# One ring of buffers for the high half, the low half and the raw form of a weight tile

## The chip, the cores and the metric

The kernel runs on 1 core of one Trainium2 chip. The metric is the device time of one execution in microseconds (us). Engines are named as the profile names them: PE is TensorE's matmul, PEld its weight load, DVE is VectorE, ACT ScalarE, POOL GpSimd, and SP is SyncE, which here only issues DMAs. A name with a q behind it (SPq, PEq) is the engine's sequencer, which waits for semaphores and issues DMAs.

## The reference

The kernel computes one layer of a streaming encoder trunk with D = 1024 for 2128 tokens (64 of a running stream, 16 meta tokens, 2048 of a prompt). Three branches (RWKV-7, S5, mLSTM) take their inputs from one combined projection:

```
P   = x @ w_in            columns shared out among the branches, their gates and the merge gates
y_b = branch_b(P columns) * silu(gate_b columns)              b in {rwkv7, s5, mlstm}
m   = sum_b sigmoid(P_merge_b + b_merge_b) * (y_b @ w_br_b)   w_br: 768, 512 and 768 rows of 1024
x   = LayerNorm(DN_ALPHA * x + m @ w_out)                     w_out: 1024 x 1024
```

Everything is float32. A product of two float32 matrices is made out of rounded parts: each operand is cut into a high part (the value rounded to the type fp32r) and a low part (the value less its high part), and three products are summed, high by high, high by low and low by high.

## The kernel before

**Weight tiles.** A weight tile is 128 columns of a weight matrix with all its rows, kept as 4, 6 or 8 k-tiles of 128 x 128 (kt below). `split_w` (line 393) makes its two parts. For each run of up to 4 k-tiles it takes three buffers: `raw`, into which SP loads the float32 columns (line 403), `hi`, which ACT writes by a rounding copy (line 404), and `lo`, which POOL writes by a subtraction (line 405). Each kind has its own ring, and the rings are counted in halves of a tile with 8 k-tiles: `WBUF` gives (3, 4) for the pool `wp` with the tag "w" (3 buffers for raw, 4 for hi, 4 for lo), and (2, 2) for the pool `gp` with the tag "g". A buffer holds 2 KB in each of 128 partitions, so the w rings take 22 KB of a partition and the g rings 12 KB.

**Token blocks.** The tokens go through five blocks: block 0 has 336 of them, the others 448 each. Each block runs 63 projections on the w rings (`proj`, which calls `load_w` at line 415 and `mm3` at 428) and 24 merge gates on the g rings (`gate_pass`, line 1499), each with kt = 8, that is 24 matmuls into one PSUM bank (tiles `d` for projections, `f` for gates). In block 0 (`first`) the tile comes from w_in by `split_w`, and hi and lo of each half are written to a DRAM buffer `wsp` (line 410, 256 KB each, so four writes for a tile). In blocks 1 to 4 `load_w` reads the four pieces back (line 424), into the hi and lo rings. `ml_gates` (line 840) builds a narrow tile on the w rings, with a raw buffer of its own, and the S5 branch loads four raw tiles of w_glu in each block into the w ring of raw buffers (line 1412).

**Merge.** `merge_pass` (line 1509) takes 768, 768 and 576 tokens. In each group it multiplies the branch outputs by w_br, 8 weight tiles each with kt = 6 (rw), 4 (s5) and 6 (ml), then by w_out, 8 tiles with kt = 8. Every one of these tiles is split afresh by `split_w`. In the last group w_out is gone through twice, for 320 and for 256 columns of tokens, so that 16 tiles are split there, with the layer norms beside them.

**What sets the order.** The branches of a block are Python generators, which `mix` steps with the weights of `MIXES` (line 1677); gate passes are given as work to fill in. From there a scheduler with a simulated timeline places the instructions of each engine, and pools hand out the buffers. All weight DMAs, raw, written and read back, are issued by SP in one queue, in order. A load into a ring waits until its buffer's last readers are done, and it keeps those behind it on SP waiting. DMAs on SP use eight semaphores in turn, so that a DMA can also wait for one eight places before it.

Of the kernel before, what the change touches and what calls it, by code (L numbers as in the profile page):

```python
# [9 lines left out]
F32 = mybir.dt.float32  # L10
F32R = mybir.dt.float32r
I32 = mybir.dt.int32
AF = mybir.ActivationFunctionType
ALU = mybir.AluOpType
# [5 lines left out]
KD = D // 128  # L20
# [63 lines left out]
def tile_trunk(ctx: ExitStack, tc: tile.TileContext, I, O, dbg=None, parts=("rw", "s5", "ml", "mg")):  # L84
    nc = tc.nc
    V, S, G, PE = nc.vector, nc.scalar, nc.gpsimd, nc.tensor
# [4 lines left out]
    dram = ctx.enter_context(tc.tile_pool(name="dram", bufs=1, space=DRAM))  # L91
    cst = ctx.enter_context(tc.tile_pool(name="cst", bufs=1))
    wp = ctx.enter_context(tc.tile_pool(name="wp", bufs=1))
# [13 lines left out]
    def pt(pool, shape, tag, dt=F32, bufs=None):  # L107
        uid[0] += 1
        kw = {} if bufs is None else {"bufs": bufs}
        return pool.tile(list(shape), dt, tag=tag, name=f"{tag}_{uid[0]}", **kw)  # L110
# [3 lines left out]
    def psum(shape, tag):  # L114
        return pt(ps, shape, tag, bufs=PSB[tag])
# [12 lines left out]
    def cut(t, off, shape):  # L128
        n = 1
        for x in shape[1:]:  # L130
            n *= x
        v = t[:shape[0], off:off + n]
        if len(shape) == 3:
            v = v.rearrange("p (a b) -> p a b", b=shape[2])
        elif len(shape) == 4:
            v = v.rearrange("p (a b c) -> p a b c", b=shape[2], c=shape[3])
        elif len(shape) == 5:
            v = v.rearrange("p (a b c d) -> p a b c d", b=shape[2], c=shape[3], d=shape[4])
        return v
# [240 lines left out]
    def load_x(b):  # L380
        for nm, j, e in (("xh", 0, nc.sync), ("xl", 1, nc.scalar)):
# [5 lines left out]

    w_in = I["w_in"][0].rearrange("(k p) c -> p k c", p=128)

    WBUF = {"w": (3, 4),  # L390
            "g": (2, 2)}

    def split_w(pool, src, kt, M, tag="w", keep=None):
        if keep is not None:
            wsp_d[keep] = pt(dram, (2, 2, 128, 4, 128), f"wsp{keep}")
        nr, nh = WBUF[tag]
        hi, lo = [], []
        for k in range(0, kt, 4):
            n = min(4, kt - k)
            h = pt(pool, (128, 4, 128), tag + "hi", F32R, bufs=nh)  # L400
            l = pt(pool, (128, 4, 128), tag + "lo", F32R, bufs=nh)
            raw = pt(pool, (128, 4, 128), tag + "raw", bufs=nr)
            nc.sync.dma_start(raw[:, :n, :M], src[:, k:k + n])
            S.copy(h[:, :n, :M], raw[:, :n, :M])  # L404
            G.tensor_tensor(l[:, :n, :M], raw[:, :n, :M], h.bitcast(F32)[:, :n, :M], ALU.subtract)  # L405
            hi += [h[:, m, :M] for m in range(n)]
            lo += [l[:, m, :M] for m in range(n)]
            if keep is not None:
                for j, t in enumerate((h, l)):
                    nc.sync.dma_start(wsp_d[keep][k // 4, j], t.bitcast(F32))  # L410
        return hi, lo

    wsp_d = {}

    def load_w(pool, off, first, tag="w"):
        nh = WBUF[tag][1]
        if first:
            wh, wl = split_w(pool, w_in[:, :, off:off + 128], KD, 128, tag, keep=off)
            return wh, wl
        hi, lo = [], []  # L420
        for k in range(0, KD, 4):
            for j, (nm, out) in enumerate((("hi", hi), ("lo", lo))):
                t = pt(pool, (128, 4, 128), tag + nm, F32R, bufs=nh)
                nc.sync.dma_start(t.bitcast(F32), wsp_d[off][k // 4, j])
                out += [t[:, m] for m in range(4)]
        return hi, lo

    def mm3(p, wh, wl, T):
# [7 lines left out]
    def proj(b, off):  # L436
        wh, wl = load_w(wp, off, b.first)
        p = psum((128, 512), "d")
        mm3(p[:, :b.T], wh, wl, b.T)
        return p  # L440
# [399 lines left out]
    def ml_gates(b):  # L840
        T = b.T
        nch = len(b.tiles)
        raw = pt(wp, (128, KD, 8), "wraw", bufs=WBUF["w"][0])
        nc.sync.dma_start(raw, w_in[:, :, O_MIF:O_MIF + 8])
        wh, wl = [], []
        for k in range(0, KD, 4):
            h = pt(wp, (128, 4, 128), "whi", F32R, bufs=WBUF["w"][1])
            l = pt(wp, (128, 4, 128), "wlo", F32R, bufs=WBUF["w"][1])
            for t in (h, l):
                G.memset(t.bitcast(F32)[:, :, 0:100], 0.0)  # L850
            for j in range(2):
                o = h[:, :, 32 * j:32 * j + 4]
                r = raw[:, k:k + 4, 4 * j:4 * j + 4]
                S.copy(o, r)
                S.copy(l[:, :, 32 * j:32 * j + 4], r)
                V.tensor_tensor(l[:, :, 64 + 32 * j:68 + 32 * j], r, o.bitcast(F32), ALU.subtract)
            wh += [h[:, m, 0:100] for m in range(4)]
            wl += [l[:, m, 0:100] for m in range(4)]
# [5 lines left out]
        li, lf, m, bb = (gr[k][:, :T] for k in ("li", "lf", "m", "b"))  # L864
# [451 lines left out]
    def s5_block(b, u_d, y_d):  # L1316
# [3 lines left out]
        for i in range(4):  # L1320
# [8 lines left out]
            for j in range(2):  # L1329
                w = cut(w5(), 0, (128, 2, 2, 128))  # L1330
# [38 lines left out]
            for q in range(4):  # L1369
                w = cut(w5(), 0, (128, 4, 128))  # L1370
                nc.sync.dma_start(w, s5wo_d[4 * i + q])
                m = []
# [3 lines left out]
                for ri in range(2):  # L1376
                    for a in range(2):
                        for g in range(2):
                            r = slice(64 * g, 64 * g + 64)
                            t = slice(64 * (a ^ g), 64 * (a ^ g) + 64)  # L1380
# [28 lines left out]
        wg = I["s5_w_glu"][0].rearrange("(k p) c -> p k c", p=128)  # L1409
        for i in range(4):  # L1410
            ch = slice(128 * i, 128 * i + 128)
            raw = pt(wp, (128, 4, 128), "wraw", bufs=WBUF["w"][0])
            nc.sync.dma_start(raw, wg[:, :, ch])
            p = psum((128, 512), "d")
            pv = p[:, :T].rearrange("p (s c) -> p s c", s=8)
            for k in range(4):
                PE.matmul(pv, raw[:, k], Gs[k], start=k == 0, stop=k == 3)  # L1417
            th = cut(sB(), 0, (128, 8, NC))
            S.activation(th, pv, AF.Tanh, scale=0.25, bias=hglu[:, i:i + 1])
            V.scalar_tensor_tensor(th, th, 1.0, Gs[i], ALU.add, ALU.mult)  # L1420
            sg = sB()
            nc.sync.dma_start(sg[:, :T], ys5_d[b.i][ch, :])
            s3 = sg[:, :T].rearrange("p (c s) -> p c s", s=8)
            V.scalar_tensor_tensor(s3, th.rearrange("p s c -> p c s"), 0.125, s3, ALU.mult, ALU.mult)
            nc.sync.dma_start(ys5_d[b.i][ch, :], sg[:, :T])
            yield
# [3 lines left out]
    def s5_stream(b):  # L1430
        for g in spend:
            yield from g
        d = yield from s5_proj(b)
        if b.first:
            yield from s5_setup()
            spend[:] = [s5_block(b, *d)]
        else:
            spend[:] = []
            yield from s5_block(b, *d)
# [69 lines left out]
    def merge_pass():  # L1509
# [58 lines left out]
        def branch_w(B, bi, d):  # L1568
            nm, yd, kt = BR[bi]
            th = pt(pool["th"], (128, TB), "th2", bufs=2)  # L1570
            for b, lo, o, m in seg[B]:
                nc.scalar.dma_start(th[:, o:o + m], g_d[b.i][D * bi + 128 * d:D * bi + 128 * d + 128, lo:lo + m])
            return split_w(wp, w_br[nm][:, :, 128 * d:128 * d + 128], kt, 128) + (th,)
# [178 lines left out]
```

## Time and profile before

| | us |
|---|---|
| median of 3 runs | 4247.48 |
| lowest, highest | 4238.52, 4260.57 |
| profiled execution | 4243.47 |
| its span in the trace | 4241.7 |

In the trace the stages are, by their windows: 0 to 100 us, start of block 0; 100 to 440 us, the larger part of block 0's weight tiles; 440 to 848 us, the end of block 0 and its change to block 1; 848 to 3600 us, blocks 1 to 4; 3600 us to the end, the merge. Busy times of PE are ends that are modelled, and matmuls follow each other closely, so the mean time of one matmul in a list is longer than its share of a row of matmuls; how long a weight tile takes PE is read from the chain of waits, which gives a time for a whole row of matmuls.

### The profile page before, as it was taken

How to read it: one execution, taken by the hardware profiler on the slowest of the kernel's cores; microseconds unless marked ns; L12 is line 12 of the kernel's file. 1: busy time of each engine (PE TensorE's matmuls, PEld its weight loads, DVE VectorE, ACT ScalarE, POOL GpSimd, SP SyncE). 2: the span in 40 equal slices, each digit the busy share in tenths (PEclk: the TensorE clock that was granted, in tenths of full speed). 3: DMA queues.
4: the chain of work that ended last, by engine and by line, in shares of the span. 5: the costliest groups of instructions: out<-in, count | busy, mean ns of one | idle time of the engine just before them, and what ended most of it. 6: DMA issues, size and time to landing. Idle time of an engine off the chain costs nothing.

```text
span 4241.7 us, 78557 instructions
## 1 busy us (share of the span) xinstructions
PE 3989.1 (94%) x27999; PEld 3427.6 (81%) x27999; DVE 2490.6 (59%) x8212; ACT 1208.0 (28%) x2655; POOL 662.9 (16%) x948
## 2 busy tenths in 40 slices
PE   6889789899999899999999999999999999999997
PEld 6778567688888778888888888878888787999997
DVE  6446886566456565556645645554665554457476
ACT  4434332232222222222322222222322222222222
POOL 5445321000000000001000000000000000233335
PEclk9999879899999899999999999999999999999999
DMA  8999647665665755656665656665566654666565
GB/s 257 332 271 320 197 136 224 175 181 187 194 211 183 226 161 175 197 181 209 196 223 165 193 173 203 178 205 189 171 202 192 168 170 132 202 194 197 156 181 165
DMA packets 803862, 834.91 MB, mean 197 GB/s; under 512 B 220246, under 2 KB 557374, under 8 KB 803470
## 3 DMA queue, kind: packets, MB, share of 16 engines
q1 hardware_dynamic: 725582, 756.61, 58.0%
q10 hardware_dynamic: 77888, 73.28, 5.8%
q8 instruction: 221, 3.62, 0.3%
q14 instruction: 171, 1.40, 0.1%
HBM read 633.92 MB, written 197.79 MB: 196 GB/s over the span
## 4 chain that ended last, share of the span: by engine, by line
PE 72%; DVE 11%; DMA 10%; SPq 2%; ACT 2%; issue 2%; POOL 1%; ACTq 0%; POOLq 0%; DVEq 0%
PE d L433 29%; PE f L433 10%; PE z L1562 7%; PE g L1562 3%; PE tr L591 2%; PE py L747 2%; PE py L744 1%; PE d L1417 1%; PE o L1011 1%; DMA ghi<-wsp 1%; DMA xT<-X 1%; DVE Ztmp L622 1%; PE tr L700 1%; PE py L734 1%; PE tr L708 1%
## 5 line engine op out<-in xcount | busy, mean ns | idle before, releaser
L433 PE MATMUL d<-xh,whi 128*128 128x448 f32 (+1 forms) x2520 | 945.9, 375 | 30.1 <-DVE zo L1092 7.7
L433 PE MATMUL d<-xh,wlo 128*128 128x448 f32 (+1 forms) x2520 | 932.4, 370 | 5.6 <-POOL wlo L405 5.1
L433 PE MATMUL d<-xl,whi 128*128 128x448 f32 (+1 forms) x2520 | 928.6, 369 | 0.0
L433 PEld LDWEIGHTS d<-xh,whi 128*128 128x128 f32 x2520 | 485.2, 193 | 86.3 <-issue 16.6
L433 PEld LDWEIGHTS d<-xh,wlo 128*128 128x128 f32 x2520 | 484.0, 192 | 55.3 <-POOL wlo L405 8.3
L433 PEld LDWEIGHTS d<-xl,whi 128*128 128x128 f32 x2520 | 485.0, 192 | 43.5 <-issue 9.1
L405 POOL TENSOR_TENSOR wlo<-wraw,whi 128x512 fp32r<-128x512 f32 (+1 forms) x310 | 397.4, 1291 | 592.7 <-ACT whi L404 541.9
L433 PE MATMUL f<-xh,ghi 128*128 128x448 f32 (+1 forms) x912 | 347.5, 381 | 39.8 <-ACT ghi L404 14.7
L433 PE MATMUL f<-xh,glo 128*128 128x448 f32 (+1 forms) x912 | 343.7, 377 | 15.8 <-POOL glo L405 9.0
L433 PE MATMUL f<-xl,ghi 128*128 128x448 f32 (+1 forms) x912 | 336.2, 369 | 0.0
L404 ACT CAST whi<-wraw 128x512 fp32r<-128x512 f32 (+1 forms) x310 | 178.9, 585 | 383.8 <-PE z L1562 97.5
L622 DVE TENSOR_TENSOR Ztmp<-Uin,Z 128x60 f32<-128x60 f32 (+24 forms) x930 | 214.4, 231 | 73.5 <-DMA Uin<-Ud 59.6
L433 PEld LDWEIGHTS f<-xh,ghi 128*128 128x128 f32 x912 | 178.2, 195 | 65.3 <-ACT ghi L404 17.0
L624 DVE TENSOR_TENSOR Z<-Z,Ztmp 128x60 f32<-128x60 f32 (+24 forms) x930 | 211.2, 227 | 14.4
L433 PEld LDWEIGHTS f<-xh,glo 128*128 128x128 f32 x912 | 178.0, 195 | 37.8 <-POOL glo L405 11.9
L1562 PE MATMUL z<-ya,whi 128*128 128x384 f32 (+1 forms) x784 | 192.2, 325 | 0.0
L433 PEld LDWEIGHTS f<-xl,ghi 128*128 128x128 f32 x912 | 178.5, 196 | 13.9 <-issue 3.1
L948 DVE SCALAR_TENSOR_TENSOR X<-X,PT 128x448 f32<-128x448 f32 (+1 forms) x180 | 124.6, 692 | 73.7 <-ACT X L946 71.4
L614 POOL MEMSET Z<- 128x256 f32 x30 | 9.4, 315 | 859.7 <-PE tr L661 443.7
L1562 PEld LDWEIGHTS z<-ya,whi 128*128 128x128 f32 x784 | 138.2, 189 | 0.4 <-issue 0.2
L747 PE MATMUL py<-XV,AT 128*64 128x64 f32 x816 | 136.4, 250 | 0.0
L1506 ACT ACTIVATE gt<-f,hbm 128x448 f32<-128x448 f32 (+1 forms) x114 | 69.8, 612 | 218.0 <-PE f L433 155.7
(725 smaller groups left out, 7304.4 us busy)
## 6 DMA issues: line engine op xcount, KB each, us to landing
whi<-wsp SPq DMA_DIRECT2D x504, 256.0 KB
wlo<-wsp SPq DMA_DIRECT2D x504, 256.0 KB
ghi<-wsp SPq DMA_DIRECT2D x192, 256.0 KB
glo<-wsp SPq DMA_DIRECT2D x192, 256.0 KB
wraw<-in_w_in_dram SPq DMA_DIRECT2D x126, 256.0 KB
wsp<-whi SPq DMA_DIRECT2D x126, 256.0 KB
wsp<-wlo SPq DMA_DIRECT2D x126, 256.0 KB
gt<-gt SPq DMA_DIRECT2D x96, 224.0 KB
```

What stands on the lines that cost most here:

```text
L404: S.copy(h[:, :n, :M], raw[:, :n, :M])
L405: G.tensor_tensor(l[:, :n, :M], raw[:, :n, :M], h.bitcast(F32)[:, :n, :M], ALU.subtract)
L433: PE.matmul(p, a[k], c, start=i == 0, stop=i == 3 * KD - 1)
L591: PE.matmul(p[:, c, :], bk[h][:, c0 + c, :], AQf[hs[h], c0 + c, :], start=True, stop=True)
L622: V.tensor_tensor(t3, Uin[:, j:j + 1, j + 1:32].to_broadcast((128, m, n)), Z[:, 0:m, j:j + 1].to_broadcast((128, m, n)), ALU.mult)
L624: V.tensor_tensor(Z[:, 0:m, j + 1:32], Z[:, 0:m, j + 1:32], t3, ALU.add)
L700: PE.matmul(p[hs[h], c], Tt[hs[h], c0 + c, :], AR[hs[h], c0 + c], start=True, stop=True)
L708: PE.matmul(p[hs[h], c], PX[hs[h], c0 + c, 0, :], AT[hs[h], c0 + c, h, :], start=True, stop=True)
L747: i = PE.matmul(py[hs[h], c, :], AT[:, c, h, 64:128], XV[:, c, h, :], start=False, stop=True, skip_group_check=True)
L948: V.scalar_tensor_tensor(acc[:, :w], raw[:, j:j + w], pcol("conv_w", 12 * j + ti), acc[:, :w], ALU.mult, ALU.add)
L1506: S.activation(t[:, :T], p[:, :T], AF.Tanh, scale=0.5, bias=hbm[:, j:j + 1])
L1562: PE.matmul(p, a[k], c[:, sl], start=i == 0, stop=i == n - 1)
```

## The change

Each ring is now one ring of buffers of 4 KB a partition, whose shape is either `pair`, (128, 2, 4, 128), the high and the low half of 4 k-tiles side by side, or `raw`, (128, 8, 128), all the raw k-tiles of a weight tile. There are five of them on "w" (20 KB a partition) and three on "g" (12 KB). `wsp` is laid out in the same way, so one DMA of 512 KB (4 KB from each partition) writes or reads a pair where two of 256 KB did. `split_w` issues both raw loads of a tile before it splits the first half. The raw tile of `ml_gates` and those of w_glu take a buffer of the w ring, and `ml_gates` clears hi and lo of a pair by one instruction. The number of weight tiles, casts, subtractions and matmuls is the same; the DMAs on SP come to 3027 where there were 3897, those on ACT's queue stay 496. In the changed file the raw load stands at line 402, the cast at 408, the subtraction at 409, the write at 413, the read back at 425, the matmul of `mm3` at 435 and the w_glu load at 1414.

```diff
--- before.py
+++ after.py
@@ -387,42 +387,44 @@
 
     w_in = I["w_in"][0].rearrange("(k p) c -> p k c", p=128)
 
-    WBUF = {"w": (3, 4),
-            "g": (2, 2)}
+    WBUF = {"w": 5, "g": 3}
+
+    def pair(pool, tag):
+        return pt(pool, (128, 2, 4, 128), tag, F32R, bufs=WBUF[tag])
 
     def split_w(pool, src, kt, M, tag="w", keep=None):
         if keep is not None:
-            wsp_d[keep] = pt(dram, (2, 2, 128, 4, 128), f"wsp{keep}")
-        nr, nh = WBUF[tag]
+            wsp_d[keep] = pt(dram, (2, 128, 2, 4, 128), f"wsp{keep}")
         hi, lo = [], []
+        raw = pt(pool, (128, 8, 128), tag, bufs=WBUF[tag])
         for k in range(0, kt, 4):
             n = min(4, kt - k)
-            h = pt(pool, (128, 4, 128), tag + "hi", F32R, bufs=nh)
-            l = pt(pool, (128, 4, 128), tag + "lo", F32R, bufs=nh)
-            raw = pt(pool, (128, 4, 128), tag + "raw", bufs=nr)
-            nc.sync.dma_start(raw[:, :n, :M], src[:, k:k + n])
-            S.copy(h[:, :n, :M], raw[:, :n, :M])
-            G.tensor_tensor(l[:, :n, :M], raw[:, :n, :M], h.bitcast(F32)[:, :n, :M], ALU.subtract)
+            nc.sync.dma_start(raw[:, k:k + n, :M], src[:, k:k + n])
+        for k in range(0, kt, 4):
+            n = min(4, kt - k)
+            t = pair(pool, tag)
+            h, l = t[:, 0], t[:, 1]
+            r = raw[:, k:k + n, :M]
+            S.copy(h[:, :n, :M], r)
+            G.tensor_tensor(l[:, :n, :M], r, h.bitcast(F32)[:, :n, :M], ALU.subtract)
             hi += [h[:, m, :M] for m in range(n)]
             lo += [l[:, m, :M] for m in range(n)]
             if keep is not None:
-                for j, t in enumerate((h, l)):
-                    nc.sync.dma_start(wsp_d[keep][k // 4, j], t.bitcast(F32))
+                nc.sync.dma_start(wsp_d[keep][k // 4], t.bitcast(F32))
         return hi, lo
 
     wsp_d = {}
 
     def load_w(pool, off, first, tag="w"):
-        nh = WBUF[tag][1]
         if first:
             wh, wl = split_w(pool, w_in[:, :, off:off + 128], KD, 128, tag, keep=off)
             return wh, wl
         hi, lo = [], []
         for k in range(0, KD, 4):
-            for j, (nm, out) in enumerate((("hi", hi), ("lo", lo))):
-                t = pt(pool, (128, 4, 128), tag + nm, F32R, bufs=nh)
-                nc.sync.dma_start(t.bitcast(F32), wsp_d[off][k // 4, j])
-                out += [t[:, m] for m in range(4)]
+            t = pair(pool, tag)
+            nc.sync.dma_start(t.bitcast(F32), wsp_d[off][k // 4])
+            hi += [t[:, 0, m] for m in range(4)]
+            lo += [t[:, 1, m] for m in range(4)]
         return hi, lo
 
     def mm3(p, wh, wl, T):
@@ -840,14 +842,13 @@
     def ml_gates(b):
         T = b.T
         nch = len(b.tiles)
-        raw = pt(wp, (128, KD, 8), "wraw", bufs=WBUF["w"][0])
+        raw = pt(wp, (128, KD, 8), "w", bufs=WBUF["w"])
         nc.sync.dma_start(raw, w_in[:, :, O_MIF:O_MIF + 8])
         wh, wl = [], []
         for k in range(0, KD, 4):
-            h = pt(wp, (128, 4, 128), "whi", F32R, bufs=WBUF["w"][1])
-            l = pt(wp, (128, 4, 128), "wlo", F32R, bufs=WBUF["w"][1])
-            for t in (h, l):
-                G.memset(t.bitcast(F32)[:, :, 0:100], 0.0)
+            t = pair(wp, "w")
+            h, l = t[:, 0], t[:, 1]
+            G.memset(t.bitcast(F32)[:, :, :, 0:100], 0.0)
             for j in range(2):
                 o = h[:, :, 32 * j:32 * j + 4]
                 r = raw[:, k:k + 4, 4 * j:4 * j + 4]
@@ -1409,7 +1410,7 @@
         wg = I["s5_w_glu"][0].rearrange("(k p) c -> p k c", p=128)
         for i in range(4):
             ch = slice(128 * i, 128 * i + 128)
-            raw = pt(wp, (128, 4, 128), "wraw", bufs=WBUF["w"][0])
+            raw = pt(wp, (128, 4, 128), "w", bufs=WBUF["w"])
             nc.sync.dma_start(raw, wg[:, :, ch])
             p = psum((128, 512), "d")
             pv = p[:, :T].rearrange("p (s c) -> p s c", s=8)
```

SP's queue in a block after block 0, before the change; `w...` tiles are projections, `g...` tiles gates, `wsp...` their place in DRAM, and PE_49 is a wait for PE, DMAHW0 to 7 for an earlier DMA:

```order
L424 DMA whi_1964_11404<-wsp4352_205_887 128x512 [waits PE_49]
L424 DMA wlo_1965_11406<-wsp4352_205_887 128x512 [waits DMAHW4_49,PE_49]
L999 DMA E_2150_12593<-rd1_105_436 128x2x128 [waits DMAHW5_49,DMAHW2_49]
L999 DMA E_2308_13546<-rd1_105_436 128x2x128 [waits DMAHW6_49]
L424 DMA ghi_2757_16353<-wsp9736_1411_8128 128x512 [waits DMAHW7_49,PE_49]
L424 DMA glo_2758_16355<-wsp9736_1411_8128 128x512 [waits DMAHW0_49,PE_49]
L424 DMA ghi_2759_16357<-wsp9736_1411_8128 128x512 [waits DMAHW1_49,PE_49]
L424 DMA glo_2760_16359<-wsp9736_1411_8128 128x512 [waits PE_49]
L1507 DMA gt1_17_97<-gt_2756_16350 128x448 [waits DMAHW3_49,Activation_49]
```

The same kind of place after the change (SP's queue):

```order
L425 DMA w_1793_11782<-wsp2816_798_5038 128x1024 [waits DMAHW3_49,PE_49]
L425 DMA w_1794_11784<-wsp2816_798_5038 128x1024 [waits DMAHW4_49,PE_49]
L425 DMA g_2376_15894<-wsp10888_1235_8104 128x1024 [waits DMAHW5_49,PE_49]
L1508 DMA gt1_17_97<-gt_2371_15859 128x448 [waits DMAHW6_49,Activation_49]
L785 DMA yrw1_7_87<-sg_1554_10161 128x448 [waits DMAHW7_49,DVE_49]
L425 DMA g_2377_15896<-wsp10888_1235_8104 128x1024 [waits DMAHW0_49,PE_49]
L425 DMA g_2380_15926<-wsp11016_1241_8144 128x1024 [waits DMAHW2_49,DMAHW1_49,PE_49]
L1508 DMA gt1_17_97<-gt_2375_15891 128x448 [waits Activation_49]
```

Where four loads of 256 KB made up a tile there are now two of 512 KB, and a gate's two pairs stand apart in the queue, with loads of other kinds between them. Each still waits for PE, which frees the buffer.

SP's queue at the first weight tiles of the merge, before; `wraw` is the raw buffer of a half tile:

```order
L403 DMA wraw_6661_40039<-in_w_br_rw_dram 128x2x128 [waits DMAHW2_49,Pool_49]
L403 DMA wraw_6667_40089<-in_w_br_rw_dram 128x4x128 [waits DMAHW4_49,Pool_49]
L403 DMA wraw_6670_40095<-in_w_br_rw_dram 128x2x128 [waits DMAHW7_49,DMAHW1_49,Pool_49]
L403 DMA wraw_6676_40145<-in_w_br_s5_dram 128x4x128 [waits DMAHW2_49,DMAHW1_49,Pool_49]
L403 DMA wraw_6685_40192<-in_w_br_s5_dram 128x4x128 [waits DMAHW4_49,Pool_49]
```

The same place after (`w` is the raw buffer of a whole tile, loaded by two DMAs):

```order
L402 DMA w_5665_38113<-in_w_br_rw_dram 128x4x128 [waits DMAHW7_49,DMAHW0_49,Pool_49]
L402 DMA w_5665_38113<-in_w_br_rw_dram 128x2x128 [waits DMAHW1_49]
L402 DMA w_5671_38166<-in_w_br_rw_dram 128x4x128 [waits DMAHW1_49,DMAHW5_49,DMAHW0_49,Pool_49]
L402 DMA w_5671_38166<-in_w_br_rw_dram 128x2x128 [waits DMAHW6_49]
L402 DMA w_5677_38219<-in_w_br_rw_dram 128x4x128 [waits DMAHW5_49,DMAHW6_49,DMAHW2_49,Pool_49]
L402 DMA w_5677_38219<-in_w_br_rw_dram 128x2x128 [waits DMAHW3_49]
L402 DMA w_5683_38272<-in_w_br_s5_dram 128x4x128 [waits DMAHW3_49,DMAHW7_49,DMAHW2_49,Pool_49]
```

Before, each half of a raw tile waits for POOL, which frees a buffer of a ring of three. Now the first half's load waits for POOL and the second half's follows it without a wait for an engine.

## Rows read from the trace of the kernel before

**Rows 1.** Part 1 of the page: busy us, share, instructions by engine.

```profile
PE 3989.1 (94%) x27999; PEld 3427.6 (81%) x27999; DVE 2490.6 (59%) x8212; ACT 1208.0 (28%) x2655; POOL 662.9 (16%) x948
```

**Rows 2.** Windows by stage: us, busy by engine, PEclk, DMA share, GB/s.

```profile
0.00:100.00 100.00, 67.04 (x350) 59.45 (x351) 65.53 (x204) 50.90 (x117) 50.76 (x103) 0.91 0.81 251
100.00:440.00 340.00, 296.62 (x2048) 267.52 (x2047) 183.88 (x555) 128.65 (x279) 164.78 (x169) 0.95 0.96 305
440.00:848.00 408.00, 336.78 (x2434) 267.11 (x2434) 300.34 (x1278) 119.70 (x328) 76.86 (x123) 0.84 0.61 181
848.00:3600.00 2752.00, 2684.18 (x19426) 2241.16 (x19424) 1565.86 (x5488) 748.26 (x1669) 144.36 (x374) 0.99 0.61 187
3600.00:4242.00 642.00, 604.50 (x3745) 592.35 (x3745) 374.93 (x689) 160.50 (x264) 226.11 (x180) 0.98 0.61 182
```

**Rows 3.** Waits of PE, whole run: total us, times, longest us.

```profile
PE f L433 <- ACT ghi L404: 14.7, 7, 5.7
PE f L433 <- DMA ghi<-wsp: 14.6, 8, 5.6
PE o L1374 <- DMA w<-s5wo: 11.7, 8, 4.3
...
PE tr L661 <- DVE Z L655: 10.9, 8, 5.4
...
PE f L433 <- POOL glo L405: 9.0, 9, 2.6
...
PE f L433 <- DMA glo<-wsp: 6.7, 6, 2.8
...
PE d L433 <- DMA whi<-wsp: 2.7, 1, 2.7
```

**Rows 4.** Chain of waits, one gate pass: start us, us, what.

```profile
1076.26 4.87 PE f L433 x24
```

**Rows 5.** Waits of SP's queue, 848 to 3600 us.

```profile
SPq L424 <- PE d L433: 712.4, 370, 8.1
SPq L424 <- PE f L433: 224.5, 122, 9.7
```

**Rows 6.** Part 3 of the page: packets, MB, share of 16 engines' span.

```profile
q1 hardware_dynamic: 725582, 756.61, 58.0%
q10 hardware_dynamic: 77888, 73.28, 5.8%
```

**Rows 7.** Line 410, 0 to 440 us: ns min/median/max, first and last start.

```profile
L410 SPq DMA_DIRECT2D wsp<-whi x88: 319/409/1152, 20.6 to 434.2; - x88
...
L410 SPq DMA_DIRECT2D wsp<-ghi x47: 319/451/1577, 79.9 to 427.7; - x47
```

**Rows 8.** DMA issues, 100 to 440 us: count, KB each.

```profile
wsp<-whi SPq DMA_DIRECT2D x70, 256.0 KB
```

**Rows 9.** Lines 404 and 405, 3640 to 4242 us.

```profile
L404 ACT CAST whi<-wraw x180: 399/620/627, 3643.8 to 4220.6; 128x512 fp32r<-128x512 f32 x134, 128x256 fp32r<-128x256 f32 x46
...
L405 POOL TENSOR_TENSOR wlo<-wraw,whi x180: 723/1291/2082, 3644.5 to 4221.2; 128x512 fp32r<-128x512 f32 x134, 128x256 fp32r<-128x256 f32 x46
```

**Rows 10.** Chain of waits, 4100 us to the end.

```profile
4112.59 47.96 PE z L1562 x360
...
4165.23 2.88 DMA wraw<-in_w_out_dram
...
4177.31 7.41 PE g L1562 x48
```

**Rows 11.** Chain of waits, start of the merge.

```profile
3633.71 134.92 PE z L1562 x768
```

**Rows 12.** Line 403, 3640 to 4242 us: SP's issue of a raw load.

```profile
L403 SPq DMA_DIRECT2D wraw<-in_w_br_ml_dram x48: 367/368/676, 3696.1 to 4147.4; - x48
```

**Rows 13.** Windows of the tail.

```profile
4161.00:4200.00 39.00, 36.75 (x257) 35.62 (x257) 20.00 (x35) 11.66 (x20) 25.70 (x20) 1.00 0.66 186
4200.00:4242.00 42.00, 21.25 (x166) 19.39 (x164) 34.00 (x91) 6.20 (x10) 14.27 (x11) 0.84 0.49 151
```


## The prediction

> **What bounds the kernel now.** I read the busy shares first: PE is busy 94% of the span, DVE 59%, POOL 16% [rows 1]. A change of buffers can gain only where PE waits for a weight. The windows by stage show where PE idles at all [rows 2]: 33 us of the first 100, 43 of the next 340, 71 of the next 408, 68 of the 2752 of blocks 1 to 4, and 37 in the merge and its tail. The stages have different limits. From 100 to 440 us the DMA engines are busy 0.96 of the time: raw tiles come in and their parts go out. From 440 to 848 DVE is the busiest beside PE (300 of 408 us) and the granted clock is 0.84; weight traffic is down to a share of 0.61. From 848 on PE is busy 97.5%, so little is left to win there. Next come PE's waits [rows 3]: 14.6 + 6.7 us on gate tiles read back from DRAM, 2.7 on one projection tile, together 24 us; 14.7 + 9.0 us on ACT's and POOL's splitting of gate tiles, which happens in block 0 alone; and waits that the change doesn't touch, as DVE's Z with 10.9 us.
>
> **Blocks 1 to 4.** A gate pass takes PE 4.87 us [rows 4]. Now the ring holds one tile: the first half of the next one is asked for when PE has done the first half of the present one, 2.43 us before it is needed. With three pairs it can be asked for at the start of the present pass, 4.87 us ahead. Each wait on a gate's half should thus shrink by up to 2.43 us. The longest waits are 5.6 and 2.8 us [rows 3]: the 2.8 falls to 0.4, the 5.6 (at the change into the merge) to 3.2, so some 4 of the 24 us stay and 20 go. But the loads stand on SP in one order, and SP is held for 712 us by projection loads that wait for PE and 225 us by gate loads [rows 5]. A gate load behind a held projection load doesn't use its earlier buffer. I take -17 us. The upper end of the gain is all 24. At the other end nothing takes a buffer that was there before: five pairs less one w_glu raw tile are still the four of now. A pair however lands as a whole, where the high half alone was enough to start. 256 KB more at the 305 GB/s of the busiest window [rows 2] are 0.86 us, times the 15 waits of these kinds: +13.
>
> **Block 0.** The writes of a tile go from four DMAs of 256 KB to two of 512 KB. Between 0 and 440 us there are 88 + 47 pairs of such writes, hi and lo [rows 7], 270 DMAs, so at 128 partitions 34,560 pieces of 2 KB become 17,280 of 4 KB. What a piece costs I estimate from the two DMA queues [rows 6]: 58.0% of 16 engines' 4241.7 us over 725,582 packets is 54.2 ns for 1043 bytes; 5.8% over 77,888 is 50.5 ns for 941 bytes. Their difference gives 0.037 ns a byte and some 16 ns for a packet of any size (5 more or less by the rounding of the shares). 17,280 x 16 ns over 16 engines is 17 us, the most that this can give. The Trainium skill's page "DMA: Bandwidth & Descriptors" ("Why small descriptors are slow") puts the fixed part at about 3 cycles of a packet beside 32 bytes a cycle, so 131 cycles for 4 KB instead of 134 for two of 2 KB; of 34,560 x (16 + 0.037 x 2048 = 92) ns / 16 = 199 us that would be an estimate of only 4 us. No row here shows 2 and 4 KB side by side.
>
> Against it stands a tie that is new. A raw tile takes a buffer of the pairs' ring, so it waits for PE and for the landing of a written pair two tiles back. The loop of two tiles is an issue of 0.37 [rows 12], a landing of 2.88 [rows 10], 0.62 and 1.29 for the casts and subtractions [rows 9], that is 5.2 us, and then the written pair's landing. 70 half tiles in 340 us [rows 8] are 9.7 us for a projection's tile, 19.4 for two, so the write may take 14 us to land before the loop binds. I count the tie at nothing; if the cover is gone, the waits on split tiles, 14.7 + 9.0 us, might come twice: +24. And what block 0's weights save is partly taken by the DVE work that bounds 440 to 848. So of the 17 I take -4, near the lower end, with -17 to +24 as bounds.
>
> **Merge.** The gain of two halves per DMA doesn't exist here, since raw loads keep their size. What changes is how far ahead they go. Before, a half tile's raw buffer was one of three. Now a kt = 6 tile needs a raw buffer and two pairs out of five, and the order shows the raw load waiting for POOL. I read this as one raw tile at a time: load, cast, subtract, next load. That chain is 0.37 + 2.88 + 0.62 + 1.29 + 0.72 (the subtraction of the two last k-tiles) = 5.9 us a tile [rows 9, 10, 12]. PE needs 134.92 / 768 = 0.176 us a matmul at 384 columns [rows 11], so 36 x 0.176 = 6.3 us for a kt = 6 tile in the first two groups: the chain is hidden. In the last group, 288 columns, it is 47.96 / 360 = 0.133 us [rows 10], 4.8 us for a tile: the chain is longer by 1.1. The eight mLSTM tiles lose 8 x 1.1 less one tile in stock, 8.6 - 4.8 = +4. The eight rw tiles stand among the norms of the group before; I count them hidden. In the tail a raw load waits for PE two tiles back: 5.2 us and half a tile. PE's tile is 24 x 7.41 / 48 = 3.7 us at 320 columns [rows 10], so the loop is 7.0 us against 7.4 for two tiles: hidden. At 256 columns it is 6.7 against 5.9, 0.4 a tile, +3 for eight, though PE is busy there only 21 of 42 us and DVE 34 [rows 13], which may hide it. So +7, between 0 (DVE hides the tail, stock covers the rest) and +44 (a landing of 4.5 us, below); less than nothing I exclude, because the load is asked for later than now.
>
> The Trainium skill ("Trainium Kernel Development and Optimization", Best Practices) says to double-buffer, so that DMA overlaps compute; it speaks against a raw tile that has the ring's last buffer. By it the load would show in every tile; by rows 9 to 12 it shows only where PE's tile is shorter than the chain, which is the rival D below.
>
> The single memset of the mLSTM gate tile, and 870 DMA issues less on SP, I cost at nothing: POOL is busy 16%, and SP's time is waiting [rows 5], not issuing.
>
> **The sum.** -17 - 4 + 7 = -14 us against the profiled execution, 4243.5: 4229.5. That execution lies 4.0 us below the median of the runs shown, 4247.5, so the forecast for a median is 4233.5, say 4234.
>
> **The rivals.**
> B, no net change, 4247. The waits on gate tiles go, and PE then waits for what stood behind them: Z from DVE (10.9), s5wo loads in SP's queue (11.7), a PSUM bank of the gates. For it speaks that SP is held by PE, so the next load is no earlier; against it, that 68 us of idle time in 2752 hold 24 of this kind and few long ones of others.
> C, a larger gain: all 24 us go and block 0 gives the whole 17, with the merge at +7: -34, so 4209.5 + 4 = 4213. For it speaks DMA at 0.96 in 100 to 440 us, and that PE waits there for split tiles; against it DVE's share after 440.
> D, slower: the raw chain of the merge. Were a raw landing 4.5 us, with the other terms as forecast, the chain would be 7.5 us. Four runs of eight kt = 6 tiles in the first two groups lose 8 x 1.2 - 6.3 = 3.3 each, 13 in all; the mLSTM run of the last group 8 x 2.7 - 4.8 = 17; the tail 4 x 1.2 + 4 x 2.4 = 14. Sum 44, total -17 - 4 + 44 = +23, so 4266.9 + 4 = 4271. It outweighs the gains from a landing of about 3.8 us on (the same sums give 20 there). For it speaks that 256 and 128 KB now come one behind the other and that other traffic takes a share of 0.66 in the tail [rows 13]; against it the 2.88 us of the chain of waits.
> That the change doesn't do what it says can be set aside: the order shows loads of 128x1024 where there were two of 128x512.
>
> **How the numbers follow.** Chances: A 0.40, B 0.12, C 0.26, D 0.22. About 0.5% (21 us) is what a measurement of this kernel can tell from no change, so faster means under 4226 and slower over 4269. A's own range is 4214 to 4248 (terms -24 to -10, -10 to +5, +3 to +15, which don't all fall one way); a third of it is below 4226, 0.13, and nearly all of C, 0.25: faster 0.38. Most of D, 0.18, and 0.01 of the rest is slower: 0.19. Same has 0.43. The range goes to 4203, ten below C, and to 4278, seven above D.
>
> **What would show it.** Right: PE's waits on gate pairs read from DRAM come to 4 to 10 us in place of 21; block 0 reaches the same work 0 to 8 us earlier, at a DMA share a little lower; in the last merge group PE waits for ACT's cast about 1 us a tile among the mLSTM tiles. Wrong: waits of PE on the cast in all groups of the merge (D); PE's idle time in 100 to 440 us far below 43 (C) or far above (the tie of the raw ring binds); blocks 1 to 4 as long as before with other waits in the list (B).

## The result and the profile after

The changed kernel took 4305.1 us in the median of 4 runs (4293.6 to 4320.6), the kernel before 4243.0 us in 4: the ratio is 1.013 (95% interval 1.010 to 1.016). It is slower by 62 us; 4234 was forecast, and 4305 lies above the range. The profiled execution took 4303.1 us with a span of 4301.3, 59.6 more than before.

Part 1 of the page after, and its windows by the same stages (columns as in [rows 2]; the last window runs to the end of the longer span):

```profile
PE 4033.6 (94%) x27999; PEld 3449.4 (80%) x27999; DVE 2485.1 (58%) x8212; ACT 1205.1 (28%) x2655; POOL 670.4 (16%) x938
```

```profile
0.00:100.00 100.00, 60.56 (x292) 55.12 (x292) 58.09 (x184) 47.11 (x108) 45.88 (x91) 0.88 0.75 237
100.00:440.00 340.00, 291.50 (x1983) 260.86 (x1983) 171.96 (x468) 124.83 (x269) 159.78 (x170) 0.93 0.91 296
440.00:848.00 408.00, 327.89 (x2255) 259.45 (x2256) 295.45 (x1310) 122.69 (x335) 84.06 (x127) 0.82 0.59 180
848.00:3600.00 2752.00, 2699.97 (x19399) 2245.74 (x19398) 1578.67 (x5508) 743.81 (x1658) 154.95 (x369) 0.98 0.60 187
3600.00:4301.00 701.00, 653.65 (x4074) 628.19 (x4072) 380.88 (x746) 166.71 (x290) 225.75 (x181) 0.98 0.59 174
```

Beside [rows 1 and 2]: over the whole run PE's idle time rises by only 15 us (span less busy, 252.6 to 267.7), its busy time by 44.5. The windows can't be set against each other as they stand, since after the change less work is done in each of the first three: 4530 matmuls up to 848 us instead of 4832. PE's waits of the whole run, after (total us, times, longest us):

```profile
PE d L435 <- ACT w L408: 40.9, 12, 8.0
...
PE o L1375 <- DMA w<-s5wo: 8.5, 10, 2.9
...
PE tr L663 <- DVE Z L657: 8.2, 5, 3.9
...
PE f L435 <- ACT g L408: 6.2, 6, 1.9
...
PE f L435 <- DMA g<-wsp: 5.4, 4, 2.2
...
PE f L435 <- POOL g L409: 5.2, 6, 2.4
```

Against [rows 3] the waits on gate pairs read back fell from 21.3 to 5.4 us, as forecast. A new one stands on top: projections (d) wait 41 us for ACT's rounding copy of their weights. What ACT waited for in the first 720 us, which hold block 0, before (first fence) and after:

```profile
ACT whi L404 <- DMA wraw<-in_w_in_dram: 10.0, 8, 2.4
...
ACT ghi L404 <- DMA graw<-in_w_in_dram: 3.8, 4, 1.8
```

```profile
ACT w L408 <- DMA w<-in_w_in_dram: 50.8, 25, 7.0
...
ACT g L408 <- DMA g<-in_w_in_dram: 17.7, 12, 4.1
```

Raw weights that used to lie ready now arrive late. One of the longest waits, in SP's queue and on ACT (start us, us, what):

```profile
306.00 0.45 SPq L413 DMA_DIRECT2D wsp<-w  x1
...
307.94 0.79 SPq L413 DMA_DIRECT2D wsp<-w  x1
308.82 1.50 SPq L402 DMA_DIRECT2D w<-in_w_in_dram  x2
```

```profile
320.85 0.62 ACT L408 CAST w<-w 128x512 fp32r<-128x512 f32 x1 [6.68 <-DMA w<-in_w_in_dram]
```

The raw load is issued at 308.8 behind two writes of pairs, and the cast starts at 320.9, when it has landed 12 us later.

In the merge, the chain of waits of the last group's mLSTM tiles was one run of PE before [rows 10]. After, PE is not in it:

```profile
4191.01 2.51 POOL w L409 x2
...
4193.53 2.90 DMA w<-in_w_br_ml_dram
...
4196.47 0.72 issue
...
4197.23 2.50 POOL w L409 x2
...
4199.74 2.99 DMA w<-in_w_br_ml_dram
...
4203.52 2.50 POOL w L409 x2
...
4206.05 4.07 DMA w<-in_w_br_ml_dram
```

Load, cast (inside the "issue" piece), two subtractions, next load: the chain of the prediction, at 6.5 us a tile (4178.4 to 4210.9 over five). The eight tiles took, before and after, in windows cut at their first and last matmul:

```profile
4122.19:4160.37 38.18, 38.18 (x290) 38.18 (x289) 21.95 (x32) 13.19 (x23) 18.86 (x15) 1.00 0.54 147
```

```profile
4172.04:4217.30 45.26, 40.21 (x291) 38.34 (x289) 18.86 (x30) 10.68 (x22) 16.99 (x14) 1.00 0.41 118
```

At a clock of 1.00 in both, 7.1 us more. PE counts as busy for 40.2 us with the same matmuls, so a little of a wait can hide in the busy column.

**Stage by stage.** Stages end at different times in different kernels, so I compare at equal work: for each trace I sum the columns that PE's matmuls move, in order of start (a matmul of fewer than 64 columns counted as 64, 7.09 million in each trace), and ask when it reaches the sum that the reference trace has at 440 us, and so on. After against before: 37 us late at 440, 30 at 690 (the end of block 0), 43 at 3640 (just behind the start of the merge), 60 at the end. Block 0 lost 30 us, the merge some 18 (its own length is 608.0 before, 626.4 after), blocks 1 to 4 the 13 between. The windows up to equal work, first before, then after:

```profile
0.00:440.00 440.00, 363.66 (x2396) 326.97 (x2396) 249.42 (x758) 179.55 (x394) 215.54 (x272) 0.94 0.92 292
0.00:690.00 690.00, 558.30 (x3736) 481.62 (x3737) 459.14 (x1667) 263.99 (x631) 286.44 (x377) 0.89 0.80 251
690.00:3633.70 2943.70, 2853.70 (x20673) 2375.17 (x20671) 1668.22 (x5884) 793.43 (x1777) 150.33 (x391) 0.98 0.61 188
```

```profile
0.00:476.50 476.50, 375.72 (x2396) 336.25 (x2396) 262.97 (x847) 182.39 (x398) 218.47 (x272) 0.91 0.86 277
0.00:719.50 719.50, 563.35 (x3671) 484.23 (x3672) 460.43 (x1681) 264.76 (x627) 283.70 (x369) 0.88 0.76 242
719.50:3674.90 2955.40, 2884.17 (x20739) 2391.32 (x20737) 1674.56 (x5873) 795.28 (x1785) 161.53 (x389) 0.98 0.60 187
```

At 440 PE has idled 24 us more and been busy 12 longer with the same matmuls, at a granted clock of 0.91 instead of 0.94. By the end of block 0 the idle time is still 24 us more (156.2 against 131.7), the busy time only 5: of the 30 us that block 0 lost, 24 are waiting. In blocks 1 to 4 PE idles 19 us less (71.2 against 90.0) and is busy 30 longer.

### The profile page after: what moved, and what is told of

The parts are those of the page before. It is cut to its first block, busy times and chain, and to the rows that moved or that the text cites. A ratio compares the mean times of both kernels' runs of the same rounds, so it can differ in the third digit from the quotient of the medians.

```text
span 4301.3 us, 76759 instructions
## 1 busy us (share of the span) xinstructions
PE 4033.6 (94%) x27999; PEld 3449.4 (80%) x27999; DVE 2485.1 (58%) x8212; ACT 1205.1 (28%) x2655; POOL 670.4 (16%) x938
## 3 DMA queue, kind: packets, MB, share of 16 engines
q14 instruction: 157, 1.29, 0.1%
## 4 chain that ended last, share of the span: by engine, by line
PE 63%; DMA 11%; DVE 6%; POOL 2%; issue 2%; SPq 1%; ACT 1%; ACTq 0%; DVEq 0%; POOLq 0%
PE d L435 26%; PE f L435 8%; PE z L1563 5%; PE g L1563 3%; DMA xT<-X 3%; PE py L749 2%; PE tr L593 2%; PE py L746 1%; PE d L1418 1%; POOL w L409 1%; PE o L1012 1%; DMA w<-s5wo 1%; PE py L736 1%; PE tr L702 1%; PE tr L710 1%
## 5 line engine op out<-in xcount | busy, mean ns | idle before, releaser
L435 PE MATMUL d<-xh,w 128*128 128x448 f32 (+1 forms) x5040 | 1537.0, 376 | 63.8 <-ACT w L408 40.9
L435 PEld LDWEIGHTS d<-xh,w 128*128 128x128 f32 x5040 | 954.4, 194 | 176.3 <-ACT w L408 47.5
L435 PE MATMUL d<-xl,w 128*128 128x448 f32 (+1 forms) x2520 | 939.0, 373 | 0.0
L435 PE MATMUL f<-xh,g 128*128 128x448 f32 (+1 forms) x1824 | 561.9, 374 | 21.9 <-ACT g L408 6.2
L435 PEld LDWEIGHTS d<-xl,w 128*128 128x128 f32 x2520 | 490.2, 195 | 45.1 <-issue 9.3
L409 POOL TENSOR_TENSOR w<-w,w 128x512 fp32r<-128x512 f32 (+1 forms) x310 | 396.6, 1292 | 650.6 <-ACT w L408 567.1
L435 PEld LDWEIGHTS f<-xh,g 128*128 128x128 f32 x1824 | 344.2, 193 | 64.9 <-ACT g L408 9.2
L435 PE MATMUL f<-xl,g 128*128 128x448 f32 (+1 forms) x912 | 335.1, 367 | 0.0
L1563 PE MATMUL z<-ya,w 128*128 128x384 f32 (+1 forms) x1168 | 210.0, 326 | 7.0 <-POOL w L409 3.6
L1563 PEld LDWEIGHTS z<-ya,w 128*128 128x128 f32 x1168 | 192.2, 189 | 10.8 <-POOL w L409 5.8
```

Of the source, the lines that this page charges most:

```text
L409: G.tensor_tensor(l[:, :n, :M], r, h.bitcast(F32)[:, :n, :M], ALU.subtract)
L435: PE.matmul(p, a[k], c, start=i == 0, stop=i == 3 * KD - 1)
L1563: PE.matmul(p, a[k], c[:, sl], start=i == 0, stop=i == n - 1)
```

## The experiments

The theory after these traces: (1) raw tiles are loaded later, because fewer raw bytes can be in flight and they share a ring with the pairs. Rivals: (2) a DMA of 512 KB that carries high and low part is itself the cost, since nothing starts until both have landed or been made; (3) the scheduler's new order costs, whatever the buffers.

The later series ran on other chips, where the kernel before has medians of 4264 to 4270 us, so only ratios within a series are compared; where an expectation gives a time, it was meant beside the 4243 us of the first pair, and I take it as a ratio to that. In the table "late" is the lateness at equal work against the trace of E5, the kernel before run in the second series, whatever chip the row's own trace comes from; "merge" is the length from its first matmul to the end; "read-back" is PE's wait on weights read from DRAM in blocks 1 to 4. All are summed from the traces. A reading 5 us to either side of 440 moves a row by up to 8 us, and which work the scheduler has put first shows there too; 690 is the firmer point, where the first trace of the kernel before and E5 differ by 2 us and those of the changed kernel by 3.

| run | w, g buffers | ratio (95%) | late at 440 / 690 | merge us | read-back us |
|---|---|---|---|---|---|
| E5 | as before | 1.0004 (0.999 to 1.0018) | 0 / 0 | 612.1 | 28 |
| E6 | as changed: w 5, g 3 shared | 1.0113 (1.0091 to 1.0135) | 36 / 28 | 628.8 | 5 |
| E1 | w 4 pairs + 3 raw, g 2 + 2 | 0.9995 (0.9976 to 1.0013) | 4 / -2 | 607.2 | 37 |
| E2 | w 4 + 3, g 3 shared | 1.0015 (1.000 to 1.0031) | 0 / 16 | 608.0 | 9 |
| E3 | w 5 shared, g 2 + 2 | 1.0103 (1.0078 to 1.0127) | 20 / 29 | 625.9 | 45 |
| E4 | w 4, g 3, 3 raw in common | 1.0065 (1.0045 to 1.0084) | 123 / 61 | 610.7 | 12 |
| E7 | w 4 + 2, g 3 shared | 1.0101 (1.0081 to 1.0121) | 29 / 18 | 627.7 | 13 |
| E8 | as E1, third gate pair in g's raw | 1.0008 (0.9995 to 1.0021) | 8 / 3 | 610.6 | 11 |
| E9 | as E6, writes by POOL | 1.0098 (1.0076 to 1.012) | 44 / 37 | 628.1 | 6 |
| E10 | as E1, writes by POOL | 1.010 (1.0081 to 1.0119) | 22 / 21 | 610.4 | 27 |
| E11 | w 3 + 4, g 3 shared | 1.0057 (1.0041 to 1.0073) | 16 / 15 | 610.9 | 24 |
| E12 | w 6 shared, g 2 + 1 | 1.0064 (1.004 to 1.0088) | 42 / -4 | 612.6 | 31 |

Raw buffers of their own are halves of 2 KB in these runs; "shared" is a ring of 4 KB as changed. Where w has raw halves of its own, the raw tiles of `ml_gates` and w_glu take those too. PE's waits on ACT and POOL for split tiles in the first 720 us, by the same traces: 32 us before and 33 in E5; 60 after, 62 in E6, 64 in E3, 56 in E7; 33 in E1, 37 in E2, 36 in E11, 35 in E12.

**E1, E2, E3: own raw rings on both, on w alone, on g alone.** The edit, with the counts of E1 (a zero leaves a ring as changed):

```diff
-    WBUF = {"w": 5, "g": 3}
+    WBUF = {"w": 4, "g": 2}
+    RAW = {"w": 3, "g": 2}
...
-        raw = pt(pool, (128, 8, 128), tag, bufs=WBUF[tag])
...
             t = pair(pool, tag)
             h, l = t[:, 0], t[:, 1]
-            r = raw[:, k:k + n, :M]
+            rh = pt(pool, (128, 4, 128), tag + "raw", bufs=RAW[tag])
+            nc.sync.dma_start(rh[:, :n, :M], src[:, k:k + n])
+            r = rh[:, :n, :M]
```

> Raw halves get rings of their own again (3 buffers on w, 2 on g), and 4 and 2 pairs are left, as much memory as before the change; hi and lo stay side by side and go in one DMA of 512 KB. If the time was lost because a raw tile in the pairs' ring is loaded later (theory 1): about the time before, 4230 to 4255 us, with ACT's waits for raw loads in the first 720 us back from 68 to about 15 us. If the 512 KB DMAs cost it (theory 2: a pair written and landing as a whole): 4285 to 4310. If it is the new order of the instructions, whatever the rings (theory 3): anywhere, with no fall of ACT's waits to go with it.

> Only the w ring gets raw buffers of its own (4 pairs, 3 raw halves); the g ring stays as changed, three buffers for pairs and raw tiles. Theory 1: faster than before the change if the third gate pair helps as the list of waits says (24 us of waits on read-back tiles became 7): 4215 to 4245, less what the gates' raw tiles lose in block 0. Theory 2: 4285 to 4310.

> The opposite: the w ring stays as changed (five buffers for pairs and raw tiles), the g ring gets 2 pairs and 2 raw halves of its own. Theory 1, with the w ring as the place (PE waited 41 us for its casts, 6 us for the gates'): 4290 to 4320, slower even than the change by what the third gate pair gave. Theory 2: the same, so this run only tells the w ring from the g ring.

Theory 2 falls: with every pair still in one DMA, E1 is as fast as before, and ACT's waits for raw loads in the first 720 us are 15 us again:

```profile
ACT w L416 <- DMA wraw<-in_w_in_dram: 8.3, 8, 2.3
...
ACT g L416 <- DMA graw<-in_w_in_dram: 3.7, 3, 1.6
...
ACT X L185 <- DMA wraw<-in_w_in_dram: 3.4, 1, 3.4
```

E3 keeps the loss and E2 nearly loses it, so the w ring is the place. Beside raw halves of its own on w, the shared g ring costs some 18 us at the end of block 0 (E2 against E1); beside the shared w ring it costs nothing there (E6 against E3). Two things didn't come as forecast: E2 was to be faster than before and is not, and E3 was to be slower than the change and is not (1.0103 of 4243 is 4287, just under its range).

**E4: one raw ring for w and g**, `rh = pt(wp, (128, 4, 128), "wraw", bufs=3)` for both tags.

> One ring of three raw halves for w and g together, beside 4 pairs on w and 3 on g. It has the third gate pair and keeps raw tiles out of the pairs. Theory 1: 4215 to 4245, if three raw halves are enough for both kinds in block 0; if not, block 0 shows ACT waiting for raw loads again and the time is 4245 to 4270. Theory 2: 4285 to 4310.

It missed the first range and lies at the upper end of the second (1.0065 of 4243 is 4271), but not by the reason given there alone: the scheduler put the gate passes of block 0 behind the projections (PE's first one starts at 591 us instead of 78), late by 123 us at 440 and by 32 at the end. Here the order does cost (theory 3), as a consequence of the buffers.

**E5, E6: the two kernels again**, without an edit, for traces side by side.

> The kernel before, unchanged, run again beside the kernel before: ratio 1.000 within 0.003. It is there for its trace, so that traces of this series can be set against a trace of the same kernel taken beside them; the clock of its executions tells how far the stages move without any change.

> The changed kernel again, in the same series: ratio 1.010 to 1.016 as before. By the traces so far, its loss lies in block 0 (about +37 us) and in the merge (about +18), and blocks 1 to 4 come out even.

E6 confirms block 0 (28 us at its end) and the merge (16.7). Between the first trace of the kernel before and E5's, blocks 1 to 4 differ by 19 us with no change at all, 14 of them in PE's busy time for the same work; differences there of less than that are not told apart by one trace.

**E7, E11: the 20 KB that the change gave w, split otherwise**, `RAW["w"]` 2 with 4 pairs, and 4 with 3 pairs.

> The w pool keeps the 20 KB that the change gave it, but split up: 4 pairs, and two raw halves in a ring of their own; g stays as changed. If what costs is that a raw tile stands in one ring with the pairs and takes a buffer whose readers are PE and a write to DRAM: ratio 1.000 to 1.004, as with three raw halves (1.0015). If what costs is that fewer raw bytes are in flight, whichever ring they stand in: 1.006 to 1.013.

> The w pool's 20 KB once more, split the other way: 3 pairs and 4 raw halves (before: 4 pairs and 2 raw halves, 1.0101); g as changed. If the raw halves in flight set the loss: merge and its tail as before the change (the tail within 3 us), block 0 at 440 us within 8 us of before, ratio 1.000 to 1.005, the rest being the waits of blocks 1 to 4 for the pair that is missing. If any smaller w pool loses the same, whichever part of it is cut: 1.008 to 1.013.

E7 goes against half of theory 1: two raw halves that share nothing with the pairs lose as much time in all as the shared ring. But the total is made of other parts, so that the two ratios are alike is in part chance. In block 0 ACT waits 80 us for raw projection tiles, PE's waits for split tiles are back (56 us, 37 with three halves), and E7 is 29 us late at 440; yet at 690 it is 18 late, where E2, with one half more, is 16 late and the shared ring 28. And the loss of the merge sits elsewhere: the eight mLSTM tiles are back at 38.7 us, the 16 tiles of the tail take 86.0 instead of 65.0. E7's two windows, then the tail before:

```profile
4166.11:4204.80 38.69, 38.46 (x290) 38.23 (x289) 20.20 (x30) 10.96 (x21) 15.75 (x14) 1.00 0.47 135
4204.80:4290.84 86.04, 66.11 (x424) 58.82 (x422) 42.78 (x91) 20.05 (x33) 41.87 (x32) 0.96 0.53 155
```

```profile
4160.37:4225.40 65.03, 58.19 (x424) 55.43 (x422) 43.75 (x89) 18.38 (x30) 40.59 (x30) 1.00 0.66 191
```

The chain gives the tail: with two halves in flight, each 0.37 + 2.88 + 0.62 + 1.29 = 5.2 us, a tile of two halves can't be faster than 5.2 us, and 86.0 / 16 is 5.4. For the mLSTM tiles it is not the limit: their full halves follow each other 5.3 us apart in E7's trace (4172.34 to 4193.71 us over four), longer than PE's 4.8, so their 38.7 us came out of tiles already split. E11, with four halves and the same memory, has tail (62.9 us) and mLSTM tiles (38.2) restored and PE's waits for split tiles in block 0 at 36 us, and is better than E7 by 0.4%. Its ratio is just above the range given and its 16 us at 440 above the 8, and at 690 it is hardly better than E7 (15 against 18), so more raw halves don't give back the end of block 0; the missing pair may cost there, which no run shows.

**E8: the third gate pair without its price.** In blocks 1 to 4 every third gate pair goes into g's two raw halves, which are idle there.

```diff
+            if tag == "g" and npair[tag] % 3 == 2:
+                h, l = (pt(pool, (128, 4, 128), "graw", bufs=RAW["g"]).bitcast(F32R) for _ in range(2))
+                for j, t in enumerate((h, l)):
+                    nc.sync.dma_start(t.bitcast(F32), wsp_d[off][k // 4, :, j])
```

> Raw rings of their own on w and g as in the run with ratio 0.9995, same memory as before the change; in blocks 1 to 4, where g loads no raw tile, every third gate pair is put into its two raw halves (as a high and a low DMA of 256 KB). If the third gate pair is worth what the waits say, and its loss elsewhere came from block 0's raw tiles alone: 0.994 to 0.998. If the waits it removes only make room for others: 0.9995 again.

The wait went, the time didn't: gate pairs cost PE 6.4 us in place of E1's 27.8, and the ratio is that of the second case. E1 first, then E8:

```profile
PE f L443 <- DMA g<-wsp: 27.8, 11, 7.8
```

```profile
PE f L451 <- DMA graw<-wsp: 6.4, 5, 2.8
```

**E9, E10: block 0's writes issued by POOL**, `nc.gpsimd.dma_start(wsp_d[keep][k // 4], ...)`, in the changed kernel and in E1.

> The changed kernel, with block 0's writes to DRAM issued by POOL, which makes the low half itself, instead of SP. SP then waits no more for POOL (95 us in its queue before a pair's write) and reaches the next raw load earlier. If raw loads are late because they stand behind those waits (theory 1a): block 0 gives back 15 to 30 of its 28 to 37 us, ratio 1.004 to 1.009. If they are late because fewer raw bytes are in flight and a raw tile waits for a buffer of a pair to be read and written out (theory 1b): block 0 as slow as before, 1.010 to 1.016, or slower by what POOL's issuing costs.

> Raw rings of their own (as in the run with ratio 0.9995) and the writes by POOL. Theory 1a: 0.993 to 0.998, since there, too, SP waits for POOL. Theory 1b: 0.998 to 1.003.

There is no sign that SP's waits for POOL are what makes raw loads late: in E9 PE waits for the cast longer than after the change (49 us against 41). The test is not a clean one, since POOL, whose subtraction frees the raw buffers, pays for the issuing: 0.57 us for each write in the median, and its busy time from 100 to 440 us, 158 in E6, is now 213:

```profile
PE d L435 <- ACT w L408: 48.7, 17, 10.5
```

```profile
100.00:440.00 340.00, 293.51 (x1970) 262.92 (x1969) 189.66 (x498) 123.70 (x268) 212.96 (x273) 0.91 0.89 290
```

E9's ratio of 1.0098 lies at the lower edge of the second range. E10 missed both ranges. It loses 21 us in block 0 and more behind it, where POOL issues none of these writes; I have no explanation for the second part.

**E12: six buffers in the shared ring**, `WBUF["w"]` 6, paid for by g's raw ring.

> The w ring shared by pairs and raw tiles as changed, but with six buffers (24 KB), two whole tiles of a raw and two pairs; to make room g gets 2 pairs and one raw half of its own (10 KB), the whole as much as before the change. If five buffers are one too few for the tile that comes next: the mLSTM tiles of the last merge group at 38 to 40 us for eight (43.7 and 45.3 with five), merge as a whole within 5 us of before, block 0 at 440 us at least 10 us better than the 28 to 37 lost; ratio 1.000 to 1.006, with what g's single raw half costs. If sharing a ring is the loss whatever its size (a raw tile waits for the readers of pairs): the mLSTM tiles stay at 42 to 45 us and the ratio at 1.009 to 1.014.

A shared ring is not the fault as such. E12 differs from E3 by the sixth buffer on w and by one raw half less on g. With two whole tiles (raw and two pairs each) in the ring, the merge is as long as in E5 and the mLSTM tiles take 38.2 us (625.9 us in E3 for the merge); block 0 is 4 us ahead at 690, where E3 is 29 late. As E12 still issues both raw loads of a w tile before it splits the first half, that order is not what costs:

```profile
4159.62:4197.81 38.19, 38.19 (x291) 38.19 (x289) 21.58 (x32) 13.30 (x24) 16.45 (x16) 1.00 0.53 152
```

At 440 us it is 42 late, against what I expected; PE waits there on ACT's cast of gate tiles (16.0 us), whose raw ring is one half here. The ratio of 1.0064, just above the range given, is not explained. By the trace it lies in blocks 1 to 4, since the merge, as long as in E5, starts 19 us later. g's raw half is not used there, and E1 has the same two gate pairs, read-back waits of 37 us against 31, and a ratio of 0.9995.

## Why the prediction was wrong

**Blocks 1 to 4 (-17).** The mechanism was right: read-back waits fell from 26 to 7 us (after) and from 28 to 5 (E6 against E5), by 19 and 23 against the 17 taken. The fear that a pair must land whole is borne out as well: with two pairs E1 and E3 wait 37 and 45 us where separate halves waited 26 and 28, 9 to 19 more, beside the bound of +13. But the gain doesn't show in the time: at equal work blocks 1 to 4 are 13 us worse in the first pair of traces and 5 better in the second, and E8 against E1 has the whole gain in the waits and nothing in the ratio. It is there in PE's idle time, 19 us less after than before (90.0 to 71.2) and 24 less in E6 than in E5 (93.2 to 68.7); but PE's busy time for the same work grew by 30 and 21 us. The windows of E5 and E6:

```profile
690.00:3651.00 2961.00, 2867.80 (x20665) 2385.94 (x20663) 1665.99 (x5885) 793.48 (x1778) 150.71 (x391) 0.98 0.62 187
```

```profile
718.40:3676.10 2957.70, 2888.95 (x20728) 2397.57 (x20726) 1672.53 (x5871) 796.09 (x1785) 160.21 (x389) 0.97 0.62 187
```

Why the busy time grew is open; between two executions of the kernel before it differs by 14 us (2853.7 and 2867.8). Rival B's outcome, no net change, held for this term, but not its mechanism: PE's idle time fell by as much as the waits that went, so other waits did not take their place.

**Block 0 (-4): the step that failed.** The prediction said "I count the tie at nothing", because two tiles take 19.4 us on average and a loop of loads and splits 5.2 plus the write. It cost 28 to 30 us at the end of the block (36 or 37 at 440), above the bound of +24. Two things in it were wrong. The 2.88 us for a raw landing came from the tail; where ACT waited for one in 100 to 440 us after the change, it was there 5.4 us after its issue in the median and up to 12.4. And a mean pace doesn't tell whether raw tiles lie ready when PE asks for them. A ring of five, which holds one tile whole and not two, brings PE's waits for split tiles to 60 to 64 us (after, E6, E3) and the end of block 0 28 to 30 us late; a ring of six, or three raw halves beside four pairs and g's own, has 33 to 35 us of such waits and block 0 as early as before (E12, E1). I had the waiting for PE and for written pairs in mind as the tie. E7, whose raw ring has neither, shows that two halves alone bring the waits for split tiles back, so depth counts. But at 690 E7 is only 2 us later than E2, with three halves, and 10 earlier than the shared ring of five: what the sharing adds beyond depth by the end of block 0 is about those 10 us. How the waits pass into lateness between 440 and 690 no run shows.

The gain from fewer, larger DMAs, bounded by 17 us, is not seen: E1, which has them in full, is at 0.9995, and its block 0 is 2 us ahead at 690. (A gain of a few us elsewhere could be hidden by E1's longer read-back waits.) The Trainium skill's fixed cost of a packet ("DMA: Bandwidth & Descriptors", "Why small descriptors are slow"), by which it would have been an estimated 4 us, fits that better than my reading of the two queues.

**Merge (+7).** The mechanism and the place were right for the mLSTM tiles of the last group; the merge as a whole lost 16.7 to 18.4 us. The chain is 6.5 us instead of 5.9, since a landing is about 3.3 us where two loads follow each other and the two subtractions end 2.5 us after the first begins, not 2.0. In the last group 8 x (6.5 - 4.8) - 4.8 gives 8.8, measured 5.6 (E6) and 7.1, against the 4 of the sum. The rest is not explained by the chain. The rw, mLSTM and w_out tiles of the first group take 8.4 us longer in E6 than in E5, though PE waits only 1.8 us there for split tiles: it waits 2.3 for a result of a branch and 2.0 for ACT's rounding of the other operand, and the rw tiles ran at a clock of 0.95 instead of 1.00. In the second group the mLSTM tiles take 49.9 us in both. That the ring of five causes the whole is shown all the same: the four traces with it have 625.9 to 628.8 us, E12 with six 612.6. What the Trainium skill says of double-buffering ("Trainium Kernel Development and Optimization", Best Practices) had the direction; the trace puts the limit to it: the load shows where PE's tile is shorter than the chain, by 6.5 against 4.8 us.

**The sum.** Rival D named the raw chain, at 4271, and put the whole of its price in the merge. The same cause, a ring too short for the next tile, acted in block 0 too, with 28 to 30 us that no rival had there, and nothing paid for it in blocks 1 to 4.

## What to carry to other kernels

When staging tiles move into the ring of the finished ones, count the ring in whole tiles, staging included: five buffers are less than two tiles of three, and the load of the next tile then starts when the split of the present one ends; a sixth buffer, or raw buffers of their own on both rings, gave back block 0 and the merge. A prefetch is priced by what lies ready when the consumer asks, with the landing time of the busiest stage, not by the mean pace and the landing of a quiet one. Two kernels are compared at equal work: by fixed windows the changed kernel shows a lower clock and less work in each of the first three, at equal work 24 of the 30 us that block 0 lost are waiting. And a wait removed from the list of an engine that is busy 97% is not yet time gained.

## What was not expected of the hardware

In the same 340 us the raw loads that ACT waited for, all of one size, took 5.4 us to land in the median and up to 12.4, the longest behind two writes of 512 KB. The matmuls of blocks 1 to 4 took PE 2853.7 us of busy time in one execution of the kernel before and 2867.8 in another. Pieces of 4 KB instead of 2 KB from each partition changed no time that these runs can tell, with an interval of 0.2% on either side.
